# A decoder block on one Trainium2 core: the last quarter of the first MLP product by the seven-product scheme

## The chip, the core and the metric

The kernel runs on one core of a Trainium2 chip. The core has five engines that run their own instruction streams: TensorE (PE in the profile, with its weight loads listed apart as PEld), VectorE (DVE), ScalarE (ACT), GpSimd (POOL) and SyncE (SP). Transfers are issued by SP, ACT and POOL and carried out by 16 DMA engines. The metric is the device time of one launch in microseconds. The time before is 901.49 us, the median of three runs (901.35 to 901.75).

## The reference

One layer of a hybrid decoder, 512 tokens of width 1024, all in float32. Two branches of token mixing (chunked gated linear attention and latent attention) are merged by gates and projected; then follows a squared-ReLU MLP of hidden width 4096:

```
g_gla, g_mla = split(sigmoid(gate_logits + b_gate))       # gate_logits: 2048 columns of h @ w_in
x = layer_norm(alpha * x + (g_gla * y_gla + g_mla * y_mla) @ w_out)
h = layer_norm(...)                                        # the MLP's input, 512 x 1024
x = layer_norm(alpha * h + square(relu(h @ w_ff1)) @ w_ff2)
```

The change touches two products: the last 1024 columns of `gate_logits`, and the last 1024 columns of `h @ w_ff1`.

## The kernel before

**Numbers.** A float32 value is held as two float32r parts, `hi` (a rounded copy, made by ACT) and `lo` (the rest, a subtraction on DVE). A product of two values is three matmuls: hi x hi, hi x lo, lo x hi. A matmul's stationary operand is a 128 x 128 tile; the moving one has up to 512 columns, and the sum goes to a PSUM bank of 128 x 512.

**Weights.** All weight tiles of 512 KB stand in one list, `stream`, in the order of use. `pump(i)`, called where tile i is used, has SP load tiles up to two ahead into a buffer `wraw` (three of them) and splits tiles up to one ahead: ACT copies into `whi` (L185), DVE subtracts into `wlo` (L186), two buffers each. Some tiles of the list come from a tile that is already on the chip (`wq`, loaded earlier, or a sum) instead of from a load.

**Order.** The program is written as generators; `spawn` starts side work, `tick` lets it advance by one step, `finish` runs it to its end. From that program a scheduler fixes the order of the instructions on each engine; an engine then executes its list in order, and waits on semaphores. A tile pool hands out buffers in turn, so an instruction that wants a buffer waits until the last reader of its previous content is done.

**Plain products.** `gemm_fm` (L238 to L240) runs over the 8 tiles of the inner dimension and for each over up to 4 output tiles of 128 columns, three matmuls of 512 tokens each. `gemm_tm` (L271 to L273) is the same with the tokens on the other side.

**Seven-product units.** A product of two matrices can be cut into 2 x 2 quadrants and done by 7 products of quadrants instead of 8, with sums of quadrants on both sides and sums of results. The last 1024 columns of the gate projection are done that way by `gemm_unit("g1")` (L1016 to L1018). Its products come in the order of `FMO`: quadrant 11, quadrant 21, sum t1, quadrant 22, sums t2, t3, t4. Each product of quadrants is 4 inner tiles x 4 output tiles x 3 = 48 matmuls of 256 columns (256 tokens). The sums of weights: t1 and t3 are made by two transfers, a load of one quadrant and, on POOL, a load that adds a second quadrant (L990); t2 and t4 are added by DVE to the tile before, as soon as the tile they add has been split (`u_sum`, L324). A weight quadrant is two tiles of the stream: tile `hf` holds half of its inner tiles, over all 512 columns. Sums of inputs come from `op_sums` (L965 to L972, splits at L111 and L112). Results are combined in `e1`, `e5` and `u2` by a copy on ACT and an addition or subtraction on DVE (L1023 to L1036).

**The MLP.** The hidden width is done in four chunks `ci` of 1024. For chunks 0 to 2 the first product is plain (`gemm_fm`, in blocks of columns), and the second is a seven-product form over 14 steps, `win_f2` (L1268 to L1270). Its weights come through POOL's queue (`win_load`, L1213) one chunk ahead. Its results are copied by ACT into `ev` (L1280) and added to the residual `res` by accumulating transfers on POOL's queue (L1282); `ev` shares a pool of 2 KB buffers with `relu`, `e1`, `e5` and `u2`. ACT's copy into `ev` therefore waits until an earlier transfer out of that buffer has landed. For chunk 3 the first product is two plain blocks of 512 columns; `ev_h` evacuates each output tile: ReLU (ACT, L1296), square into the high part (ACT, L1310), the square again in float32 (POOL, L1311), the difference as the low part (DVE, L1312). Then the last second product, `f2last`, runs as `gemm_tm` with the last layer norm behind it.

Of the kernel before, what the change touches and what calls it, by code (L numbers as in the profile page):

```python
# [19 lines left out]
P = 128  # L20
T = 512
# [31 lines left out]
def tile_hybrid_block(ctx: ExitStack, tc: tile.TileContext, I, out, dbg=None):  # L53
# [108 lines left out]
    def pump(i):  # L162
        while st["dma"] < min(len(stream), i + 1 + DMA_AHEAD):
# [10 lines left out]
            e["raw"] = raw  # L174
        while st["spl"] < min(len(stream), i + 2 + SPLIT_AHEAD):
            e = stream[st["spl"]]
            if st["spl"] > i + e.get("ahead", SPLIT_AHEAD) and not e["res"]:
                break
            nk, n = e["nk"], e["n"]
            hi, lo = [A([P, nk, T * 2 // nk], F32R, w) for w in HOME["a" if e["res"] else e.get("home", "w")]]  # L180
            raw = e["src"]() if "src" in e else e.pop("raw")
            with ExitStack() as gates:
                for g in st["gates"]:
                    gates.enter_context(tc.issue_after(g.ins))
                st["ins"] = act(hi[:, :nk, :n], raw[:, :nk, :n], AF.Copy)  # L185
                vtt(lo[:, :nk, :n], raw[:, :nk, :n], f(hi[:, :nk, :n]), op=ALU.subtract)  # L186
# [121 lines left out]
    UNITS = {"g1": ("w_in", C_G + D)}  # L308

    def plan_src(key, seq, homes):  # L310
        PL[key] = []
# [10 lines left out]
    def u_sum(key, a, to, hf, x):  # L322
        t = WQ[key, (to, hf)] = WQ[key, (a, hf)]
        vtt(t, t, x, op=ALU.add)  # L324


    for key in UNITS:
        PL[key] = []
        for op, _ in FMO:
            for hf in range(2):  # L330
                PL[key].append(len(stream))
                e = {"nk": 2, "n": T, "res": False}
                if op[0] != "t":
                    e["dmas"] = [(slice(0, 2), u_src(key, int(op[0]) - 1, int(op[1]) - 1, hf), None)]
                else:
                    e["src"] = lambda q=(key, (op, hf)): WQ[q]
                if op == "22":
                    e["post"] = lambda raw, q=(key, "t1", "t2", hf): u_sum(*q, raw)
                elif op == "t2":
                    e["post"] = lambda raw, q=(key, "t2", "t4", hf): u_sum(*q, WQ[key, ("21", q[3])])  # L340
                stream.append(e)
    plan_qr(0)
    PL["yg", 0] = plan("w_o_gla", 0, T)

# [22 lines left out]


    FC = 4
    F1 = [((0, 4), (4, 2), (6, 2))] + [tuple((b, 2) for b in range(0, 8, 2))] * 2 + [((0, 4), (4, 4))]  # L370
    WIN = (("11", 0, 0), ("21", 0, 1), ("11", 1, 0), ("21", 1, 1), ("T1", 0, 2), ("T1", 1, 2), ("T2", 0, 3), ("T2", 1, 3),
           ("T4", 0, 4), ("T4", 1, 4), ("22", 0, 5), ("22", 1, 5), ("T3", 0, 6), ("T3", 1, 6))
    fb = 0
    for ci in range(FC):
        nb = 8
        for b, w in F1[ci]:
            PL["f1", ci, b] = plan("w_ff1", (fb + b) * P, w * P, res=(ci == 0 and b == 0), per=8 // w)
        if ci < FC - 1:
            plan_src(("f2", ci), [(op, hf) for op, hf, _ in WIN], HOMES)
        else:  # L380
            plan_zip("f2last", [("w_ff2", 0, fb, True), ("w_ff2", T, fb, True)])
        fb += nb

# [598 lines left out]
            yield  # L982
            ops.append(o)

    def u_load(key, op):
        for hf in range(2):
            t = WQ[key, (op, hf)] = A([P, 2, T], F32, "wq")
            nc.sync.dma_start(t, u_src(key, *{"21": (1, 0)}.get(op, (0, 1)), hf))
            if op != "21":
                nc.gpsimd.dma_start(t, u_src(key, *{"t1": (0, 0), "t3": (1, 1)}[op], hf), accum_op=ALU.add)  # L990

    def gemm_unit(key, ops, evac, after=None):

        bank, e1, e5, u2 = {}, {}, {}, {}
        nk = 2
        for n, (op, ph) in enumerate(FMO):
            items = PL[key][2 * n:2 * n + 2]
            for g in range(2):
                bk = ("a" if ph in (0, 3, 6, 4) else "b", g)
                opens = ph in (0, 2, 1)  # L1000
                if opens:
                    bank[bk] = (PX if ph == 1 else MM)()
                o = bank[bk]
                for hf, it in enumerate(items):
                    pump(it)
                    hi, lo = stream[it]["w"]
                    for pp in range(nk):
                        while len(ops) <= nk * hf + pp:
                            tick(3)
                        xh, xl = ops[nk * hf + pp][ph]  # L1010
                        for a in range(2):
                            c = slice((2 * g + a) * P, (2 * g + a + 1) * P)
                            oa = o[:, a * 256:(a + 1) * 256]
                            first = opens and hf == 0 and pp == 0 and a == 0
                            last = hf == 4 // nk - 1 and pp == nk - 1
                            mm(oa, hi[:, pp, c], xh, start=first, stop=False, skip_group_check=True)  # L1016
                            mm(oa, hi[:, pp, c], xl, start=False, stop=False, skip_group_check=True)  # L1017
                            mm(oa, lo[:, pp, c], xh, start=False, stop=last, skip_group_check=True)  # L1018
                        if pp % 2:
                            tick(3)  # L1020
                if ph == 0:
                    e1[g] = B([P, T], F32, "e1")
                    act(e1[g], o, AF.Copy)  # L1023
                elif ph == 1:
                    vtt(e1[g], o, e1[g], op=ALU.add)
                    evac(0, 0, g, e1[g], None)
                elif ph == 2:
                    e5[g] = B([P, T], F32, "e5")
                    act(e5[g], o, AF.Copy)
                elif ph == 3:  # L1030
                    u2[g] = B([P, T], F32, "u2")
                    act(u2[g], o, AF.Copy)
                    vtt(u2[g], bank["b", g], u2[g], op=ALU.subtract)
                    evac(1, 0, g, u2[g], None)
                elif ph == 6:
                    vtt(e5[g], e5[g], o, op=ALU.subtract)  # L1036
                    evac(1, 1, g, e5[g], None)
                elif ph == 4:
                    evac(0, 1, g, o, None)
            if after:  # L1040
                after(op)


    gt = [None] * NK
# [207 lines left out]
    def win_f2(ci, hid):  # L1252
        bank = {}
        for n, (op, hf, ph) in enumerate(WIN):
# [27 lines left out]
                        nc.gpsimd.dma_start(res[tt + t][:, j * T:(j + 1) * T], e, accum_op=ALU.add)  # L1282
            if n == 9 and ci + 1 < FC - 1:
                win_load(ci + 1)

    WT = {}
    for ci in range(FC):
        nb = 8
        hid = []
# [4 lines left out]
        def ev_h(a, ps):  # L1294
            r = B([P, T], F32, "relu")
            act(r, ps, AF.Relu)  # L1296
            if win:
                if a % 2 == 0:
                    hid.append({"R": A([P, 2, T], F32, "hr")})
                ops = hid[-1]  # L1300
                R = ops["R"]
                act(R[:, a % 2, :], r, AF.Square)
                if a % 2:
                    h1 = A([P, 2, 2, 256], F32R, "h1p")
                    split(R[:, :, :256], h1[:, 0], h1[:, 1])
                    ops[0], ops[1] = [(h1[:, 0, i], h1[:, 1, i]) for i in range(2)]
                    spawn(win_hid(R, ops))
                return
            hh = A([P, 2, T], F32R, "hid0")
            act(hh[:, 0, :], r, AF.Square)  # L1310
            gtt(r, r, r, op=ALU.mult)  # L1311
            vtt(hh[:, 1, :], r, f(hh[:, 0, :]), op=ALU.subtract)  # L1312
            hid.append(hh)
        for b, w in F1[ci]:
            if ci == 0 and b == 0:
                gemm_fm(PL["f1", ci, b], h1T, T, ev_h, toks=slice(256, T), accs=accs)
# [11 lines left out]
            win_f2(ci, hid)  # L1328
        else:
            bg, bb = bcast_row("ln2_g"), bcast_row("ln2_b")  # L1330
            gemm_tm(PL["f2last"], hid, T, ev_res, tts=(0, 1))
            spawn(ln2(0))
            spawn(ln2(1))
# [65 lines left out]
```

## Time and profile before

| what | value |
|---|---|
| median of the runs | 901.49 us (901.35 to 901.75) |
| the profiled execution's own time | 901.97 us |
| its span | 900.2 us |
| instructions | 12161 |
| PE busy | 880.9 us, 98% of the span, 4652 matmuls |
| DVE, ACT, POOL busy | 585.5, 427.3, 178.0 us |

The profile lists each instruction with its start and duration in microseconds of the span, what ended the idle time before it, and what it read and wrote under the program's tile names. Matmuls are pipelined, so that a matmul's listed duration is longer than the distance to the next one's start; distances between starts give the rate. In a row of a group, the number behind x is the count, then follow busy time and mean. `res<-ev` is a transfer from the tile ev to the tile res. "To landing" is the time from a transfer's issue to the end of its last packet. In the list of before, the gate unit runs from 274 to 318 us, the second product of chunk 2 ends at 805 us, the first product of chunk 3 runs from 805 to 848.5 us, and `f2last` begins there.

### The profile page before, as it was taken

The page shows a single profiled execution, that of the slowest core. Times are in us where ns is not written, and L with a number is a line of the kernel's source. Part 1 is how long each engine was busy: PE and PEld are TensorE (multiplying, and loading weights), DVE is VectorE, ACT ScalarE, POOL GpSimd, SP SyncE. Part 2 cuts the span into 40 slices and gives each one's busy share as a digit, 9 for nine tenths or more (in the row PEclk, how much of TensorE's full clock was granted, in tenths as well). Part 3 has the DMA queues.
Part 4 walks back from the last instruction along what each step waited for, and adds up shares of the span by engine and source line. Part 5 has one row for each costly group of instructions (what it writes and reads, how often), then busy time and mean ns, then how long its engine had stood idle before and what let it go on. Part 6 is the DMA issues. An engine that isn't in the chain of part 4 may idle for free.

```text
span 900.2 us, 12161 instructions
## 1 busy us (share of the span) xinstructions
PE 880.9 (98%) x4652; PEld 755.8 (84%) x4652; DVE 585.5 (65%) x953; ACT 427.3 (47%) x729; POOL 178.0 (20%) x196
## 2 busy tenths in 40 slices
PE   5999999999999999999999999999999999999996
PEld 5988888888889988888888888988888888888885
DVE  7835855577876645747756797997557646723565
ACT  5556443443546543445644423466367546733410
POOL 0103442444531010100000002104400520142200
PEclk9999999999999999999999999999999999999999
DMA  7414323216225623121207518005941990594311
GB/s 241 124 47 159 129 65 94 71 47 155 81 71 195 175 88 105 43 60 53 94 24 277 191 49 302 1 1 151 296 115 32 261 243 24 117 209 108 128 68 73
DMA packets 64776, 107.25 MB, mean 119 GB/s; under 512 B 7840, under 2 KB 27680, under 8 KB 64720
## 3 DMA queue, kind: packets, MB, share of 16 engines
q1 hardware_dynamic: 51344, 75.57, 26.3%
q0 software_dynamic: 11456, 27.27, 13.0%
q10 hardware_dynamic: 1920, 3.66, 1.2%
q8 instruction: 36, 0.59, 0.3%
q14 instruction: 20, 0.16, 0.1%
HBM read 89.18 MB, written 4.72 MB: 104 GB/s over the span
## 4 chain that ended last, share of the span: by engine, by line
PE 96%; DVE 2%; DMA 1%; ACT 1%; issue 0%; SPq 0%; DVEq 0%
PE mm L238 14%; PE mm L240 14%; PE mm L239 14%; PE mm L271 7%; PE mm L273 7%; PE mm L272 7%; PE px L1269 2%; PE px L1270 2%; PE px L1268 2%; PE px L723 2%; PE mm L1269 2%; PE mm L1270 2%; PE mm L1268 2%; PE mm L1018 1%; PE mm L1016 1%; PE mm L1017 1%
## 5 line engine op out<-in xcount | busy, mean ns | idle before, releaser
L186 DVE TENSOR_TENSOR wlo<-wraw,whi 128x1024 fp32r<-128x1024 f32 (+1 forms) x102 | 115.3, 1131 | 131.6 <-ACT whi L185 124.0
L185 ACT ACTIVATE whi<-wraw 128x1024 fp32r<-128x1024 f32 (+1 forms) x102 | 98.2, 962 | 109.5 <-PE mm L239 63.3
L238 PE MATMUL mm<-h,whi 128*128 128x512 f32 x352 | 137.6, 392 | 0.0
L239 PE MATMUL mm<-h,whi 128*128 128x512 f32 x352 | 137.3, 390 | 0.0
L240 PE MATMUL mm<-h,wlo 128*128 128x512 f32 x352 | 130.5, 390 | 0.0
L1282 POOL DMA_DIRECT2D res<-ev x48 | 42.1, 1018 | 187.5 <-ACT ev L1280 151.6
L238 PEld LDWEIGHTS mm<-h,whi 128*128 128x128 f32 x352 | 66.0, 188 | 13.5
L240 PEld LDWEIGHTS mm<-h,wlo 128*128 128x128 f32 x352 | 66.0, 188 | 13.5
L239 PEld LDWEIGHTS mm<-h,whi 128*128 128x128 f32 x352 | 66.1, 188 | 13.3
L272 PE MATMUL mm<-wlo,h 128*128 128x512 f32 x128 | 50.3, 393 | 0.0
L273 PE MATMUL mm<-whi,h 128*128 128x512 f32 x128 | 50.1, 392 | 0.0
L271 PE MATMUL mm<-whi,h 128*128 128x512 f32 x128 | 49.7, 403 | 0.0
L185 ACT ACTIVATE xh<-wraw 128x1024 fp32r<-128x1024 f32 (+1 forms) x28 | 27.1, 985 | 36.8 <-PE mm L273 16.5
L662 POOL TENSOR_TENSOR rp<-rp 128x256 f32<-128x256 f32 x32 | 31.6, 987 | 61.2 <-ACT E L667 44.8
L1296 ACT ACTIVATE relu<-mm 128x512 f32<-128x512 f32 x32 | 18.8, 595 | 49.3 <-PE mm L240 49.2
L186 DVE TENSOR_TENSOR wlo<-wq,whi 128x1024 fp32r<-128x1024 f32 x20 | 24.5, 1225 | 24.2 <-ACT whi L185 24.2
L391 POOL TENSOR_TENSOR mv<-mv,mhalf 128x1 f32<-128x1 f32 x4 | 4.6, 1154 | 172.4 <-DVE mv L390 172.4
L186 DVE TENSOR_TENSOR xl<-wraw,xh 128x1024 fp32r<-128x1024 f32 (+1 forms) x28 | 31.2, 1128 | 8.9 <-ACT xh L185 8.7
L669 DVE TENSOR_TENSOR M<-E,qk 128x512 f32<-128x512 f32 x32 | 27.8, 868 | 14.1 <-ACT E L667 14.1
L667 ACT ACTIVATE E<-rp 128x512 f32<-128x512 f32 x32 | 20.4, 638 | 24.9 <-POOL rp L663 24.9
L663 POOL TENSOR_TENSOR rp<-rp 128x256 f32<-128x256 f32 x32 | 28.2, 883 | 8.9 <-ACT q L692 6.7
L273 PEld LDWEIGHTS mm<-whi,h 128*128 128x128 f32 x128 | 24.0, 188 | 5.0
(405 smaller groups left out, 2415.3 us busy)
## 6 DMA issues: line engine op xcount, KB each, us to landing
wraw<-in_w_ff_dram SPq DMA_DIRECT2D x40, 512.0 KB, 4.5
wraw<-in_w_in_dram SPq DMA_DIRECT2D x38, 512.0 KB, 3.5
wq<-in_w_ff_dram POOLq DMA_DIRECT2D x24, 512.0 KB, 9.4
res<-ev POOLq DMA_DIRECT2D x48, 256.0 KB, 6.6
wraw<-in_w_o_gla_dram SPq DMA_DIRECT2D x8, 512.0 KB, 3.8
wraw<-in_w_o_mla_dram SPq DMA_DIRECT2D x8, 512.0 KB, 3.5
wraw<-in_w_out_dram SPq DMA_DIRECT2D x8, 512.0 KB, 3.9
wq<-in_w_in_dram SPq DMA_DIRECT2D x6, 512.0 KB, 5.5
```

Of the source, the lines that this page charges most:

```text
L185: st["ins"] = act(hi[:, :nk, :n], raw[:, :nk, :n], AF.Copy)
L186: vtt(lo[:, :nk, :n], raw[:, :nk, :n], f(hi[:, :nk, :n]), op=ALU.subtract)
L238: mm(o, hi[:, c], xh, start=first, stop=False)
L239: mm(o, hi[:, c], xl, start=False, stop=False)
L240: mm(o, lo[:, c], xh, start=False, stop=last)
L271: mm(o, xh, hi[:, :n], start=opens, stop=False, skip_group_check=share)
L272: mm(o, xh, lo[:, :n], start=False, stop=False, skip_group_check=share)
L273: mm(o, xl, hi[:, :n], start=False, stop=last, skip_group_check=share)
L1268: mm(o, xh[:, c], hi[:, pp], start=opens, stop=False, skip_group_check=True)
L1269: mm(o, xh[:, c], lo[:, pp], start=False, stop=False, skip_group_check=True)
L1270: mm(o, xl[:, c], hi[:, pp], start=False, stop=hf == 1 and pp == 1, skip_group_check=True)
L1282: nc.gpsimd.dma_start(res[tt + t][:, j * T:(j + 1) * T], e, accum_op=ALU.add)
```

## The change

Three things change.

1. In a seven-product unit a weight quadrant's two tiles are now its two column halves (`g`), each with all four inner tiles, loaded in rows of 1 KB instead of 2 KB. A tile then serves 24 matmuls into one output bank, and the next tile the other bank. The sums of weights on DVE are put behind the last low-half subtraction queued before them (`issue_after(st["lo"].ins)`).
2. The last chunk's first product is done by a unit "f1" of the same form: 336 matmuls of 256 columns in the place of 192 of 512. Its input sums are made by `op_sums` on `h1T`, spawned in step 10 of the third `win_f2`. In the same `win_f2` POOL issues the two transfers for t1 in step 8, SP is told to fetch up to quadrant 22 in step 9, and POOL loads quadrant 21 in step 11. That quadrant is kept, and DVE adds it to t2 for t4 instead of loading it again. The transfers for t3 are issued on POOL after product 21.
3. The evacuation of that chunk, `ev_u`, does its float32 square on DVE instead of POOL, in generators that step beside the products; `Halves` lets `f2last` wait for each quarter of the hidden tile.

```diff
-    def u_src(key, i, j, hf):
-        return src[:, 4 * hf + i:4 * hf + i + 3:2, c0 + j * T:c0 + (j + 1) * T]
+    def u_src(key, i, j, g):
+        c0 += j * T + g * 256
+        return src[:, i:8:2, c0:c0 + 256]
...
+        with tc.issue_after(st["lo"].ins):
+            vtt(t, t, x, op=ALU.add)
...
-    F1 = [((0, 4), (4, 2), (6, 2))] + [tuple((b, 2) for b in range(0, 8, 2))] * 2 + [((0, 4), (4, 4))]
+    F1 = [((0, 4), (4, 2), (6, 2))] + [tuple((b, 2) for b in range(0, 8, 2))] * 2 + [()]
...
+            plan_unit("f1")
...
+            for g in range(2):
+                bk = ("a" if ph in (0, 3, 6, 4) else "b", g)
+                o, it = bank[bk], PL[key, op, g]
+                pump(it)
+                hi, lo = stream[it]["w"]
+                for k in range(4):
+                    xh, xl = ops[k][ph]
+                    for a in range(2):
+                        c = slice(a * P, (a + 1) * P)
+                        oa = o[:, a * 256:(a + 1) * 256]
+                        mm(oa, hi[:, k, c], xh, start=opens and k == 0 and a == 0, stop=False, skip_group_check=True)
+                        mm(oa, hi[:, k, c], xl, start=False, stop=False, skip_group_check=True)
+                        mm(oa, lo[:, k, c], xh, start=False, stop=k == 3, skip_group_check=True)
...
+            if ci == FC - 2 and n == U0:
+                t_h1.append(spawn(h1_sums()))
+            if ci == FC - 2 and n == U2:
+                fetch(PL["f1", "22", 0] + 1)
+            if ci == FC - 2 and n == U1:
+                u_load("f1", "t1", nc.gpsimd.dma_start)
+            if ci == FC - 2 and n == U3:
+                u_load("f1", "21", nc.gpsimd.dma_start)
...
+    U0, U1, U2, U3 = 10, 8, 9, 11
...
-            hh = A([P, 2, T], F32R, "hid0")
-            act(hh[:, 0, :], r, AF.Square)
-            gtt(r, r, r, op=ALU.mult)
-            vtt(hh[:, 1, :], r, f(hh[:, 0, :]), op=ALU.subtract)
...
+            def ev_u(j, i, g, ps, sb):
+                def later():
+                    for _ in range(1 + 4 * i):
+                        yield
+                    r = ps if sb else B([P, T], F32, "relu")
+                    act(r, ps, AF.Relu)
+                    hh = A([P, 2, 2, 256], F32R, "hid0")
+                    act(hh[:, 0], r.rearrange("p (a c) -> p a c", a=2), AF.Square)
+                    yield
+                    vtt(r, r, r, op=ALU.mult)
+                    vtt(hh[:, 1], r.rearrange("p (a c) -> p a c", a=2), f(hh[:, 0]), op=ALU.subtract)
+                    hts[j, i, g] = hh
+                spawn(later())
+            def after1(op):
+                if op == "21":
+                    u_load("f1", "t3", nc.gpsimd.dma_start)
+            gemm_unit("f1", hops, ev_u, after1)
```

More of the change, by code (lines that the diff above doesn't have):

```diff
@@ L1001, in gemm_unit @@
                 if opens:
[L1002 to L1020, printed above, removed]
+                    bank[bk] = (PX if ph == 1 else (pb or MM) if ph == 2 else MM)()
@@ L1296, in ev_h @@
             act(r, ps, AF.Relu)
[L1297 to L1308, printed above, removed]
-            hh = A([P, 2, T], F32R, "hid0")
[L1310 to L1313, printed above, removed]
+            if a % 2 == 0:
+                hid.append({"R": A([P, 2, T], F32, "hr")})
+            ops = hid[-1]
+            R = ops["R"]
+            act(R[:, a % 2, :], r, AF.Square)
+            if a % 2:
+                h1 = A([P, 2, 2, 256], F32R, "h1p")
+                split(R[:, :, :256], h1[:, 0], h1[:, 1])
+                ops[0], ops[1] = [(h1[:, 0, i], h1[:, 1, i]) for i in range(2)]
+                spawn(win_hid(R, ops))
         for b, w in F1[ci]:
```

90 lines of the change are left out of this document (58 added, 32 removed).

## The prediction

> **What bounds the kernel.** I read the page's busy shares and slices first, then the chain that ended last, then windows around the two places that the change touches.
>
> ```profile
> PE 880.9 (98%) x4652; PEld 755.8 (84%) x4652; DVE 585.5 (65%) x953; ACT 427.3 (47%) x729; POOL 178.0 (20%) x196
> ...
> PE   5999999999999999999999999999999999999996
> ...
> PEclk9999999999999999999999999999999999999999
> ...
> PE 96%; DVE 2%; DMA 1%; ACT 1%; issue 0%; SPq 0%; DVEq 0%
> ```
>
> PE is busy 98% of the span, in every slice but the first and last, at full clock, and 96% of the chain is PE. So the time follows the PE time of the work, plus any gap that another engine forces into it. The profiled execution took 901.97 us for a span of 900.2 us (1.8 us lie around it), 0.48 us above the median of 901.49 us. I work out a difference in the span and take it from the median.
>
> ```profile
> 775.00:805.00 30.00, 30.00 (x134) 24.85 (x133) 15.72 (x14) 16.05 (x22) 10.37 (x12) 1.00 0.92 202
> 805.00:849.00 44.00, 44.00 (x196) 36.42 (x194) 14.64 (x12) 15.46 (x23) 9.04 (x9) 1.00 0.48 132
> 849.00:893.00 44.00, 43.53 (x215) 36.87 (x213) 30.81 (x46) 8.06 (x10) 7.73 (x7) 1.00 0.20 72
> ```
>
> The columns are the length, then the busy time of PE, PEld, DVE, ACT and POOL, the clock, the DMA share and GB/s. The tail of the third second-MLP product (775 to 805), the first product's last 1024 columns (805 to 849) and the start of the last product have no idle PE. A shorter first product is thus gained in full if its operands come in time. DVE, ACT and POOL have about half their time or more free until 849, but the DMA engines are 92% busy before 805.
>
> **1. Fewer, narrower matmuls.** PE rows of both shapes, start and duration, and the weight loads of the narrow ones:
>
> ```profile
> 805.02 0.39 PE L238 MATMUL mm<-h,whi 128*128 128x512 f32 x1
> ...
> 806.38 0.39 PE L238 MATMUL mm<-h,whi 128*128 128x512 f32 x1
> ...
> 285.86 0.28 PE L1016 MATMUL px<-h,whi 128*128 128x256 f32 x1
> ...
> 287.06 0.28 PE L1016 MATMUL px<-h,whi 128*128 128x256 f32 x1
> ...
> L1018 PEld LDWEIGHTS mm<-h,wlo x32: 186/192/192, 274.4 to 317.7; 128*128 128x128 f32 x32
> ```
>
> Durations overlap, so starts are what counts. Six starts of 512 columns lie in 805.02 to 806.38: 0.2267 us each. Ten of 256 columns lie in 285.86 to 287.06: 0.120 us each. The old form is 2 blocks x 4 row tiles x 8 input tiles x 3 = 192 matmuls: 43.5 us, as the window shows. The new one is 7 products x 48 = 336 matmuls: 40.3 us. **Term: -3.2 us.** Seven eighths of the arithmetic would be -5.4 us; the narrow form gives back 2.2 us of it (0.120 against 0.113).
>
> The Trainium skill (TensorE: Matmul & The Clock Gate, section Back-to-back issue gap) gives sustained spacings of about 81 ns at 128 columns and 131 ns at 512 for streams with a weight load per matmul. Interpolated, 256 columns would take some 98 ns, an estimate from that page, and this term would turn to 336 x 0.098 - 192 x 0.131 = +7.8 us. The rows above differ on both widths, and they decide.
>
> **2. The gate unit's split by columns.** PE and DVE around the unit's only real gap:
>
> ```profile
> 311.53 0.28 PE L1017 MATMUL mm<-h,whi 128*128 128x256 f32 x1
> 312.29 0.38 PE L1018 MATMUL mm<-h,wlo 128*128 128x256 f32 x1 [0.48 <-DVE wlo L186]
> ...
> 310.41 0.69 DVE L1036 TENSOR_TENSOR e<-e,mm 128x512 f32<-128x512 f32 x1 [1.87 <-PE mm L1018]
> 311.01 1.22 DVE L186 TENSOR_TENSOR wlo<-wq,whi 128x1024 fp32r<-128x1024 f32 x1
> ```
>
> The matmul that should start 0.12 us after 311.53 starts at 312.29, 0.64 us late, and the next one 0.10 us later than the pace: 0.74 us. It waited for the low half of the next weight tile (wlo, 311.01 + 1.22). DVE runs in order, and that subtract stood behind e (L1036), which waited 1.87 us for the whole product to end. Split by rows, a product's two outputs end together. Split by columns, the first ends after 24 matmuls, 2.88 us earlier than the second; e (0.69) and the subtract (1.22) then fit before the next tile is needed. **Term: -0.7 us**, between -0.74 and 0. The weight sums stand behind the last subtract instead of ahead of it, so they delay nothing. Loads now have 1 KB rows instead of 2 KB; the accumulating ones are costed below. Nothing else in the unit moves.
>
> **3. More work on ACT and DVE.**
>
> ```profile
> L186 DVE TENSOR_TENSOR wlo<-wraw,whi 128x1024 fp32r<-128x1024 f32 x82 | 103.1, 1258 | 111.5 <-ACT whi L185 103.9 <-PE px L817 3.6 <-PE px L880 3.4
> L185 ACT ACTIVATE whi<-wraw 128x1024 fp32r<-128x1024 f32 x82 | 86.8, 1059 | 82.7 <-PE mm L239 43.1 <-PE mm L273 14.1 <-DMA wraw<-in_w_ff_dram 6.8
> ...
> L1221 DVE TENSOR_TENSOR T<-wq,wq 128x1024 f32<-128x1024 f32 x12 | 14.5, 1220 | 0.9 <-DMA wq<-in_w_ff_dram 0.9
> ...
> L965 DVE TENSOR_TENSOR hraw<-h 128x512 f32<-128x512 f32 x8 | 6.2, 803 | 0.0
> ...
> L112 DVE TENSOR_TENSOR sh<-hx,sh 128x512 fp32r<-128x512 f32 x8 | 5.7, 740 | 3.1 <-ACT sh L111 3.1
> ...
> L1311 POOL TENSOR_TENSOR relu<-relu 128x512 f32<-128x512 f32 x8 | 10.3, 1301 | 35.4 <-ACT hid L1310 35.4
> L1312 DVE TENSOR_TENSOR hid<-relu,hid 128x512 fp32r<-128x512 f32 x8 | 10.3, 1312 | 11.8 <-POOL relu L1311 11.8
> ...
> L1296 ACT ACTIVATE relu<-mm 128x512 f32<-128x512 f32 x8 | 4.8, 595 | 8.6 <-PE mm L240 8.4
> ...
> L1036 DVE TENSOR_TENSOR e<-e,mm 128x512 f32<-128x512 f32 x2 | 1.4, 686 | 1.9 <-PE mm L1018 1.9
> ```
>
> Columns are count, then busy us, mean ns, idle before. The new unit splits 14 weight tiles where 8 were split: 6 more at 1.26 on DVE and 1.06 on ACT. DVE adds four weight sums (the shape of L1221, 1.22 each), eight sums of inputs (L965, 0.80), sixteen half-width ones (about half that, 0.4), eight low halves (0.74), six combinations like L1036 (0.69) and eight squares taken over from POOL, where L1311 took 1.30; on DVE a tensor operation of that shape takes 0.69. The subtract L1312 stays; its 1.31 was taken beside POOL's multiply, so it may shrink toward 0.69. In sum 7.6 + 4.9 + 6.4 + 6.4 + 5.9 + 4.1 + 5.5 = 41 us more DVE work, beside 15.7 + 14.6 = 30.3 us busy in the 74 us from 775 to 849. That is 96%, though a part of the evacuation falls behind 845. ACT gains 6.4 (splits) + 4.8 (input sums) + 3.6 (copies of banks) = 15 us on 31.5 and stays far from full. A tile is used for 24 x 0.120 = 2.88 us, and its successor needs ACT 1.06 and DVE 1.26 in turn, 0.56 us less. The gate unit kept this pace with the same kinds of work, and its one gap is that of step 2. I take **0**; the high end is 0.5 us for four of the products, +2 us.
>
> **4. The POOL queue: the unknown.** The new loads go through POOL's queue, among the accumulating copies of ev into res (L1282). Its order after the change, from 785 on: the base of t1, both halves; two copies; then POOL waits for the first base to land and issues its accumulate, quadrant "21" in two halves, a copy, the other accumulate, a copy (the pair that began at 791.15 before), eight more issues of copies, and last the base and the accumulates of t3. No form with both was run. Rows: copies when the queue is light; 512 KB loads and copies when it is full; accumulating loads.
>
> ```profile
> 784.90 0.86 POOL L1282 DMA_DIRECT2D res<-ev  x1 [1.71 <-ACT ev L1280]
> ...
> 791.15 0.86 POOL L1282 DMA_DIRECT2D res<-ev  x1 [0.85 <-ACT ev L1280]
> ...
> DMA to landing us min/median/max: 3.3/5.0/7.5
> ...
> DMA to landing us min/median/max: 7.1/10.5/13.2
> ...
> 644.13 0.60 ACT L1280 ACTIVATE ev<-mm 128x512 f32<-128x512 f32 x1 [1.19 <-DMA res<-ev]
> 645.91 0.60 ACT L1280 ACTIVATE ev<-px 128x512 f32<-128x512 f32 x1 [1.18 <-DMA res<-ev]
> 647.69 0.60 ACT L1280 ACTIVATE ev<-px 128x512 f32<-128x512 f32 x1 [1.19 <-DMA res<-ev]
> ...
> 287.62 2.54 POOL L990 DMA_DIRECT2D wq<-in_w_in_dram  x2 [8.45 <-PE px L1018]
> ...
> DMA to landing us min/median/max: 8.5/9.3/10.1
> ```
>
> The full queue (622 to 652) lands things in issue order. Eight loads issued 622.7 to 630.3 land 7.1 to 13.2 us after issue, and copies land so that ev, which waits for the buffer of an earlier one, runs at 644.13, 645.91, 647.69: 1.78 us for each piece. Two accumulates issued together at 287.62, 1.27 us apart, took 8.5 and 10.1 us: the second landed about 2.9 us behind the first. Here the last earlier copy (issued 784.90) lands some 3.5 us later, at 788.4, near the light queue's 3.3. Ten pieces then follow, up to the second copy of that pair: 8 x 1.75 + 2 x 2.9 = 19.8, so it lands at 808.2.
>
> Its buffer is what the last ev of this second product waits for, whose matmuls end at 805.02. ACT is in order: behind this ev (0.60) stand half of an input's split (0.6) and the high half of "21", first column half (1.06). So ACT finishes at 810.5 and DVE's low half at about 811.8. PE reaches "21" after 48 x 0.120 us, at 810.8, and its third matmul, the first with the low half, at 811.0. **Term: +1.2 us** (0.8 by this sum, and 0.4 for four steps from engine to engine), between 0 (1.4 us per piece: landing at 803.8) and +3.0 (3.5 us per accumulate and POOL held until a base lands late: 810.4).
>
> The second deadline is t3. Its base is issued when the copies before it have their buffers, about 812, lands by 824, and the accumulates land about 830 and 833. ACT wants the halves by 833.8 - 2.3 = 831.5 and 834.4, later by any earlier stall. That is a cover of 1 us: cost 0, and 1 to 2 us if the queue is slower by a tenth.
>
> SP's own loads are not moved past anything, but they share the engines. Of the first row below (the whole run) and the other two (630 to 652), the last column is the median time to landing:
>
> ```profile
> wraw<-in_w_ff_dram SPq DMA_DIRECT2D x40, 512.0 KB, 4.5
> ...
> res<-ev POOLq DMA_DIRECT2D x11, 256.0 KB, 10.2
> wraw<-in_w_ff_dram SPq DMA_DIRECT2D x3, 512.0 KB, 11.2
> ```
>
> SP's 512 KB loads took 11.2 us there instead of 4.5. The Trainium skill (Trainium Kernel Development and Optimization, Key Constraints) says that all queues use the same 16 DMA engines and interleave; this row agrees. Loads of "11" are issued by about 786 and wanted near 797 and 802, those of "22" by 801 for 819, so 11 us is still hidden. Those of the last product are issued as each split tile frees its buffer, about one product (5.76 us) ahead: with 4.5 us the cover is about 1 us, and a late one would cost what it is late. One load of "21" instead of two saves transfers, not time.
>
> **5. The rest.** f2last reads the new halves as they are made; evacuation of the last output (ACT 0.6 + 0.6, DVE 0.69 + 0.69) ends about 848, and f2last uses it last, so 0. LN2 and the output transfers follow PE unchanged.
>
> **Sum:** -3.2 - 0.7 + 0 + 1.2 = -2.7 us: 899.3 for an execution like the profiled one, **898.8 us** against the median.
>
> **Rivals.**
> - Full gain: the queue is quick enough and ACT never waits. -3.2 - 0.7: 897.6 us. For it: in the light queue copies land 3.3 to 7.5 us after issue. Against it: six 512 KB loads come on top.
> - Pace: the split chain loses 0.3 to 0.6 us in most products, or the gate unit gains nothing. For it: DVE at 96%, cover of 0.56 us. Against it: the gate unit's single gap. -3.2 + 1.2 + 2 to 3: 900 to 902.5 us, no change.
> - Slower, the queue's backlog. If a piece takes 2.2 us and an accumulate 3 or more, that copy lands at 812 to 815; "21" stalls 4.5 to 7.5 us, and t3, behind ten more pieces, costs 2 to 4 us more. -3.9 + 6.5 to 11.5: 904 to 909 us. It decides from a landing past 809.5 on. For it: DMA already at 92%. Against it: 1.78 in the fullest stretch of this run.
> - Weight loads set the pace of narrow matmuls: LDWEIGHTS takes 0.192 us, more than the 0.120. 336 x 0.19 = 64 us, +20 us: 922 us. Against it: the 0.120 us starts with those very loads.
>
> **How the numbers follow.** Forecast with a stall of 0.3 to 2.1 us (897.9 to 899.7): 0.44. Full gain: 0.13. Pace: 0.2. Backlog: 0.21. Weight loads: 0.02. What a measurement can tell from no change is about 0.2%, 1.8 us: faster 0.57 (the first two), same 0.2, slower 0.23. The range runs from 897.2 (full gain, less the 0.4 us between the lowest and the highest of the runs shown) to 904, where the backlog begins; 0.2 is left out above it. The forecast's own range is 897.6 to 899.9.
>
> **What would show it.** Step 1: starts 0.120 us apart over 40.3 us, no 512-column matmul from 805 to 845. Step 2: no PE gap near 311, e runs before wlo. Step 3: no PE gap put down to DVE wlo within the unit, DVE above 80% there. Step 4: the first matmuls of "21" near 811 wait about 1 us for wlo or whi, whose ACT stood behind ev waiting for DMA res<-ev; t3's high half waits for no DMA. The prediction is wrong if that copy lands past 810, if t3's accumulates land past 834, or if PE shows gaps at every second tile.

## The result, and the profile after

The changed kernel takes 906.35 us, the median of 6 runs (905.37 to 909.06); the kernel before, on the same chip, 901.42 us (6 runs, 900.98 to 901.75). The ratio is 1.0060, with an interval of 1.0045 to 1.0076: slower by 4.9 us, where 2.7 us faster was forecast. The profiled execution took 905.63 us for a span of 903.5 us, 3.3 us more span than before. What follows explains that one execution; it lies 0.7 us below the median.

The page of the changed kernel, its busy shares, clock and chain:

```profile
PE 879.5 (97%) x4796; PEld 761.3 (84%) x4796; DVE 617.3 (68%) x1009; ACT 440.2 (49%) x749; POOL 178.1 (20%) x198
...
PE   6999999999999999999999999999999999988996
...
PEclk9999999999999999999999999999999999998999
...
PE 92%; DMA 4%; DVE 2%; issue 1%; ACT 1%; POOL 0%; SPq 0%; DVEq 0%; POOLq 0%; ACTq 0%
```

PE has less work and is no longer busy throughout: two more slices of 22.6 us show a digit below 9, one of them at a lower clock. On the chain, DMA has gone from 1% to 4%. The same place in windows (columns as before: length, busy time of PE, PEld, DVE, ACT, POOL, clock, DMA share, GB/s):

```profile
775.00:805.00 30.00, 30.00 (x140) 25.09 (x139) 26.61 (x41) 16.86 (x25) 14.13 (x16) 1.00 0.93 217
805.00:809.30 4.30, 4.30 (x38) 4.24 (x36) 1.85 (x3) 0.60 (x1) 0.85 (x1) 1.00 1.17 231
809.30:815.20 5.90, 0.14 (x2) 0.00 (x0) 0.69 (x1) 2.04 (x4) 0.85 (x1) 0.76 1.12 251
815.20:819.20 4.00, 3.46 (x14) 3.17 (x15) 3.06 (x3) 2.46 (x5) 3.51 (x6) 0.50 1.09 194
819.20:852.00 32.80, 32.80 (x266) 32.34 (x265) 27.91 (x31) 21.82 (x29) 4.15 (x4) 1.00 0.61 136
```

Nearly all of the loss lies in 10 us. PE stands still from 809.3 to 815.2, between quadrant 11 and quadrant 21, and then works for 4 us at a granted clock of 0.50. The matmuls there, and ACT's row of instructions that PE waited for:

```profile
809.16 0.28 PE L1023 MATMUL mm<-h,wlo 128*128 128x256 f32 x1
815.27 0.58 PE L1021 MATMUL px<-h,whi 128*128 128x256 f32 x1 [5.83 <-ACT whi L188]
815.66 0.41 PE L1022 MATMUL px<-h,whi 128*128 128x256 f32 x1
816.53 0.58 PE L1023 MATMUL px<-h,wlo 128*128 128x256 f32 x1 [0.46 <-DVE wlo L189]
...
817.56 0.41 PE L1021 MATMUL px<-h,whi 128*128 128x256 f32 x1
817.77 0.41 PE L1022 MATMUL px<-h,whi 128*128 128x256 f32 x1
...
819.23 0.28 PE L1023 MATMUL px<-h,wlo 128*128 128x256 f32 x1
```

```profile
806.62 0.60 ACT L1291 ACTIVATE ev<-px 128x512 f32<-128x512 f32 x1 [3.07 <-PE mm L1023]
813.16 0.60 ACT L1291 ACTIVATE ev<-px 128x512 f32<-128x512 f32 x1 [5.94 <-DMA res<-ev]
813.66 0.62 ACT L111 ACTIVATE sh<-hx 128x512 fp32r<-128x512 f32 x1
814.18 1.05 ACT L188 ACTIVATE whi<-wq 128x1024 fp32r<-128x1024 f32 x1
```

The copy that the last `ev` waited for:

```profile
L1293 POOL DMA_DIRECT2D res<-ev x1: 2144/2144/2144, 798.4 to 798.4; - x1
...
DMA to landing us min/median/max: 14.6/14.6/14.6
```

It is the place that step 4 named. The last `ev` of the second product waits 5.94 us for a buffer, that is, for an earlier copy into `res` to land: it was issued at 798.45 and landed at 813.08, 0.08 us before this `ev` starts. The `ev` before it, at 806.62, also starts 0.08 us after such a landing (806.54), so its 3.07 us were most likely the same wait, though the profile names PE. Half of an input's split and the high half of "21" stand behind it on ACT, and PE stands behind those. Quadrant "21" itself had been on the chip since 805.3 us by the trace.

The account of the span: the gate unit starts at 273.60 instead of 274.32, so 0.7 us are won in the part ahead that the change does not touch (in the profile of experiment 7's control, which does not have the change, it starts at 273.80, so most of it is a difference between executions). The gate unit itself is 0.8 us shorter (42.81 against 43.58 from its first matmul to the next stage), and the first product's matmuls 3.2 us. Against that, the gaps beyond the pace between 760 and 903 add up to 8.3 us: 6.0 of standstill, 0.75 for the low half at 816.53, 1.3 for starts 0.21 us apart instead of 0.120 until 819.23, and 0.3 between the first two matmuls after the standstill. Another -0.3 is what the other terms leave over: -0.7 - 0.8 - 3.2 + 8.3 - 0.3 = +3.3 us.

### The profile page after: what moved, and what is told of

It is laid out like the page before. It is cut to its first block, busy times and chain, and to the rows that moved or that the text cites. A ratio compares the mean times of both kernels' runs of the same rounds, so it can differ in the third digit from the quotient of the medians.

```text
span 903.5 us, 12536 instructions
## 1 busy us (share of the span) xinstructions
PE 879.5 (97%) x4796; PEld 761.3 (84%) x4796; DVE 617.3 (68%) x1009; ACT 440.2 (49%) x749; POOL 178.1 (20%) x198
## 4 chain that ended last, share of the span: by engine, by line
PE 92%; DMA 4%; DVE 2%; issue 1%; ACT 1%; POOL 0%; SPq 0%; DVEq 0%; POOLq 0%; ACTq 0%
PE mm L241 12%; PE mm L243 12%; PE mm L242 12%; PE mm L274 7%; PE mm L275 7%; PE mm L276 7%; DMA res<-ev 2%; PE mm L1022 2%; PE mm L1023 2%; PE mm L1021 2%; PE px L1280 2%; PE px L1279 2%; PE px L1281 2%; PE px L731 2%; PE mm L1280 1%; PE mm L1279 1%
## 5 line engine op out<-in xcount | busy, mean ns | idle before, releaser
L189 DVE TENSOR_TENSOR wlo<-wraw,whi 128x1024 fp32r<-128x1024 f32 (+1 forms) x98 | 110.4, 1127 | 108.6 <-ACT whi L188 101.0
L241 PE MATMUL mm<-h,whi 128*128 128x512 f32 x288 | 112.7, 392 | 0.0
L242 PE MATMUL mm<-h,whi 128*128 128x512 f32 x288 | 112.4, 390 | 0.0
L243 PE MATMUL mm<-h,wlo 128*128 128x512 f32 x288 | 107.1, 390 | 0.0
L243 PEld LDWEIGHTS mm<-h,wlo 128*128 128x128 f32 x288 | 53.9, 188 | 11.1
L241 PEld LDWEIGHTS mm<-h,whi 128*128 128x128 f32 x288 | 54.0, 188 | 11.0
L242 PEld LDWEIGHTS mm<-h,whi 128*128 128x128 f32 x288 | 54.1, 188 | 10.8
L189 DVE TENSOR_TENSOR wlo<-wq,whi 128x1024 fp32r<-128x1024 f32 x30 | 36.7, 1224 | 19.9 <-ACT whi L188 19.8
L670 POOL TENSOR_TENSOR rp<-rp 128x256 f32<-128x256 f32 x32 | 31.7, 990 | 61.1 <-ACT E L675 44.8
L188 ACT ACTIVATE whi<-wq 128x1024 fp32r<-128x1024 f32 x30 | 31.7, 1057 | 19.6 <-PE mm L1022 10.8
L1021 PE MATMUL mm<-sh,whi 128*128 128x256 f32 x128 | 36.2, 283 | 0.0
L1022 PE MATMUL mm<-sh,whi 128*128 128x256 f32 x128 | 36.2, 283 | 0.0
L1023 PE MATMUL mm<-sh,wlo 128*128 128x256 f32 x128 | 36.2, 283 | 0.0
```

Source lines behind the costliest of these rows:

```text
L189: st["lo"] = vtt(lo[:, :nk, :n], raw[:, :nk, :n], f(hi[:, :nk, :n]), op=ALU.subtract)
L241: mm(o, hi[:, c], xh, start=first, stop=False)
L242: mm(o, hi[:, c], xl, start=False, stop=False)
L243: mm(o, lo[:, c], xh, start=False, stop=last)
L1021: mm(oa, hi[:, k, c], xh, start=opens and k == 0 and a == 0, stop=False, skip_group_check=True)
L1022: mm(oa, hi[:, k, c], xl, start=False, stop=False, skip_group_check=True)
```

## The experiments

The theory after the result was: the copies of the third second product land late in a queue that now carries six more loads, and ACT waits for their buffers. The rivals: the accumulating loads are what is slow; the order on POOL's queue is; or DVE's load would hold the pace below the forecast even without this stall.

**1. The gate unit alone.** The last 1024 columns of the first MLP product stay plain; only the split by columns and the place of the sums are kept. The old evacuation, with the square on POOL, is back too.

```diff
-    F1 = [((0, 4), (4, 2), (6, 2))] + [...] * 2 + [()]
+    F1 = [((0, 4), (4, 2), (6, 2))] + [...] * 2 + [((0, 4), (4, 4))]
...
-            plan_unit("f1")
...
```

> The gate unit split by columns, the last chunk's first product plain as before. Theory (the loss is all in the new unit, from the POOL queue): the gap of 0.74 us near 311 is gone and nothing else moves, so 901.4 - 0.7 = 900.7 us. Rival (the 1 KB rows or the moved weight sums cost something in the gate unit): 901.4 or more.

Measured: 901.07 us (11 runs, 900.46 to 901.68) against 901.72, ratio 0.9993 (0.9985 to 1.0002); span 899.2. The -0.65 us is the size of step 2, but its interval holds 1: the time alone does not show it. The trace of the changed kernel does. Its matmuls at the place of the old gap run at the pace:

```profile
311.37 0.28 PE L1021 MATMUL mm<-h,whi 128*128 128x256 f32 x1
...
311.97 0.28 PE L1023 MATMUL mm<-h,wlo 128*128 128x256 f32 x1
```

Five steps in 0.60 us, with no wait. The loss thus belongs to the unit "f1", with its loads and its evacuation.

**2. The loads on SP's queue.** The bases of t1 and t3 and quadrant "21" go through SP's queue; the accumulating loads have to stay on POOL's.

```diff
-                u_load("f1", "t1", nc.gpsimd.dma_start)
+                u_load("f1", "t1")
...
-                u_load("f1", "21", nc.gpsimd.dma_start)
+                u_load("f1", "21")
...
-                    u_load("f1", "t3", nc.gpsimd.dma_start)
+                    u_load("f1", "t3")
```

> As changed, but the plain loads of the new unit (bases of t1 and t3, quadrant 21) are issued on SP's queue; only the accumulating loads stay on POOL's. Theory (it is the order of POOL's queue that makes the copy before the last ev land late, 813 us): four loads fewer stand ahead of that copy, about 4 x 1.75 = 7 us, it lands near 806, the stall at quadrant 21 falls from 7 us to under 2, and the time is 898 to 901 us. Rival (the 16 DMA engines are full in that stretch, whatever the queue): the copy still lands past 811 and the time stays at 904 to 907 us.

**3. The same, without the accumulating loads.** The sums t1 and t3 then hold one quadrant only.

```diff
-            if op != "21":
+            if op != "21" and key != "f1":
                 nc.gpsimd...
```

> As the run before with the loads on SP, and without the new unit's four accumulating loads, so t1 and t3 hold one quadrant each and the output is not the reference's. POOL's queue carries only the copies, as before the change. Theory (queue): no stall is left, 901.4 - 0.7 - 3.2 = 897.5 us. Rival (DVE at 96% or the split chain cannot keep 2.88 us per tile): gaps at wlo remain, and the time is 899 us or more.

Measured: 903.28 us (10 runs, 900.44 to 905.03; ratio 1.0016, 1.0005 to 1.0027) and 903.33 us (10 runs, 900.68 to 905.15; 1.0014, 1.0005 to 1.0023). Both win 3 us on the changed kernel, and the second wins nothing on the first: with the other loads on SP's queue, the accumulating loads cost nothing that the time shows. Experiment 2 was expected at 898 to 901 us and experiment 3 at 897.5; both came out slower. In experiment 2 the copy that had landed at 813.1 landed at 807.1, as its theory of the queue's order has it (near 806), and the stall at "21" fell to 1.0 us. But PE stood still at another place, 798 to 800.4, in both. PE and ACT in experiment 3, which has neither accumulating loads nor new loads on POOL's queue:

```profile
798.00 0.39 PE L1279 MATMUL px<-whi,xh 128*128 128x512 f32 x1
800.43 0.50 PE L1280 MATMUL px<-wlo,xh 128*128 128x512 f32 x1 [2.05 <-DVE wlo L189]
800.77 0.40 PE L1281 MATMUL px<-whi,xl 128*128 128x512 f32 x1
801.01 0.48 PE L1279 MATMUL px<-whi,xh 128*128 128x512 f32 x1
801.29 0.63 PE L1280 MATMUL px<-wlo,xh 128*128 128x512 f32 x1
801.72 0.63 PE L1281 MATMUL px<-whi,xl 128*128 128x512 f32 x1
```

```profile
783.54 0.60 ACT L1291 ACTIVATE ev<-px 128x512 f32<-128x512 f32 x1 [3.23 <-DMA res<-ev]
784.03 1.05 ACT L188 ACTIVATE xh<-T 128x1024 fp32r<-128x1024 f32 x1
...
792.45 0.60 ACT L1291 ACTIVATE ev<-mm 128x512 f32<-128x512 f32 x1 [3.20 <-DMA res<-ev]
792.94 1.05 ACT L188 ACTIVATE xh<-wq 128x1024 fp32r<-128x1024 f32 x1
```

`ev` waits for copies here too, three times around 3 us from 783 on (3.23, 2.61 and 3.20), and each time a split `xh` stands behind it. DVE idles for `xh` as long (2.93 us before its row at 789.27, 3.52 before 794.02); the input sums for "f1" then come late in DVE's order, and the low half that PE wants at 798.2 is begun only at 799.16. The three copies issued from 780.6 to 788.6 land 7.0 to 7.9 us after issue; the three from 782.3 to 787.3 in the kernel before took 3.5 to 6.2 us. New in this stretch are the 512 KB loads on SP's queue, so these delay POOL's copies too. Changing the queue moved the place of the stall and cut the loss against the kernel before from 4.9 to 1.6 us. The rival of experiment 3, that DVE cannot hold the pace, named the place where PE waits (`wlo`) and the time (899 us or more), but not the reason: DVE had idled for ACT.

**4. The copies replaced by additions on POOL.** The 16 results of that second product are added into `res` by POOL as a tensor operation.

```diff
-                        nc.gpsimd.dma_start(res[...], e, accum_op=ALU.add)
+                        if ci == FC - 2:
+                            gtt(rr, rr, e, op=ALU.add)
+                        else:
+                            nc.gpsimd.dma_start(rr, e, accum_op=ALU.add)
```

> As changed, all loads on POOL's queue, but the third second product's copies into the residual are additions by POOL (16 of 128x512, about 1.3 us each by POOL's multiply) instead of accumulating transfers. Theory (ACT waits for a copy's landing, not the weights for theirs): ev is free 1.3 us after it is written, quadrant 21 is on the chip near 800, no stall at 811, 897.5 to 899 us. Rival 1 (the weights themselves are late): the stall stays above 4 us. Rival 2 (POOL's additions slow DVE, which is nearly full): gaps at wlo of 0.5 us per product, 900 to 903 us.

Measured: 915.17 us (4 runs, 912.66 to 915.56), ratio 1.0142 (1.0128 to 1.0156). No `ev` waits for a transfer any more, but DVE became slow. Groups of POOL and DVE from 775 to 812 in this run, and then those of DVE in the changed kernel:

```profile
L1295 POOL TENSOR_TENSOR res<-res,ev 128x512 f32<-128x512 f32 x12 | 21.9, 1840 | 51.7 <-ACT ev L1291 51.7
...
L189 DVE TENSOR_TENSOR xl<-wq,xh 128x1024 fp32r<-128x1024 f32 x2 | 5.3, 2702 | 0.0
L112 DVE TENSOR_TENSOR sh<-hx,sh 128x512 fp32r<-128x512 f32 x4 | 4.9, 1226 | 0.0
...
L980 DVE TENSOR_TENSOR hx<-hraw 128x256 f32<-128x256 f32 x3 | 3.8, 1251 | 0.0
```

```profile
L112 DVE TENSOR_TENSOR sh<-hx,sh 128x512 fp32r<-128x512 f32 x6 | 3.9, 686 | 0.3 <-ACT sh L111 0.2
...
L189 DVE TENSOR_TENSOR xl<-wq,xh 128x1024 fp32r<-128x1024 f32 x2 | 2.4, 1222 | 0.0
...
L980 DVE TENSOR_TENSOR hx<-hraw 128x256 f32<-128x256 f32 x4 | 1.7, 419 | 0.0
```

These operations take 2.70 us in the mean instead of 1.22, 1.23 instead of 0.69, 1.25 instead of 0.42; some other groups of the window did not grow (the sums of L973 take 0.68 in both). PE then waited for ACT and DVE at six places, 10.7 us together. The time lies above everything expected: the second rival had the mechanism, at 900 to 903 us. This run says nothing on the copies, but on where such an addition must not be done. The Trainium skill (SBUF — State Buffer, section SBUF: two separate sides) says that DVE with two SBUF inputs and a GpSimd operation share a pair of ports as a lock held for the whole instruction; rows that grow, by less than the 1.84 us that one addition of POOL's takes, agree with that.

**5. No copies at all.** The copies of that second product are left out (its results are missing in the output); every load stays as it is in the changed kernel.

```diff
-                        nc.gpsimd.dma_start(res[...], e, accum_op=ALU.add)
+                        if ci < FC - 2: nc.gpsimd.dma_start(res[...], e, accum_op=ALU.add)
```

> As changed, with the third second product's 16 copies into the residual left out (ev is still written, nothing reads it, and the output lacks that product). All loads of the new unit stay on POOL's queue. Theory (the copies fill queue and engines, and through ev's buffers hold ACT and then DVE): no gap near 800 or 811, and 901.4 - 0.7 - 3.2 = 897.5 us. Rival (DVE's input sums, or the loads by themselves, are late): a gap of 2 us or more at wlo or whi remains, 900 us or more.

Measured: 897.35 us (4 runs, 897.23 to 897.55) against 901.5, ratio 0.9954 (0.9939 to 0.9968). The window over what was the stall (columns as above):

```profile
803.50:847.00 43.50, 43.50 (x352) 42.92 (x351) 36.48 (x43) 28.54 (x39) 2.59 (x2) 1.00 0.43 109
```

PE has no gap, at full clock, with DVE at 84%. This is the price of the rival "full gain" (-3.2 - 0.7: 897.6) to 0.3 us. The copies of the third second product, or the wait for them, are the cause, and steps 1 to 3 hold with the pace as forecast. Whether it is their volume on the DMA engines or the wait of `ev` for their landing, this run cannot tell; experiments 6 and 9 can.

**6. Three pairs of results added by DVE.** Where step 5, 7 or 9 of the 14 ends (the results T1, T2 and T4), DVE adds the PSUM bank into `res`; `ev` and the copies of these six results go, the other ten remain.

```diff
+                    if ci == FC - 2 and n in (5, 7, 9):
+                        for tt, j in (...)[ph]:
+                            rr = res[tt + t][:, j * T:(j + 1) * T]
+                            vtt(rr, rr, o, op=ALU.subtract if ph == 4 else ALU.add)
+                        continue
                     e = B([P, T], F32, "ev")
```

> As changed, but in the third second product the results T1, T2 and T4 are added to the residual by DVE straight from the PSUM bank (6 x 0.69 us), so that ACT writes 6 ev fewer and POOL's queue has 6 copies fewer; the four of the first two products, quadrant 22's two and T3's four stay transfers. Theory: ev's buffers are free when wanted, quadrant 21's copy-bound stall goes, the time is 897.5 to 899 us. Rival (DVE, nearly full, is the bound as soon as ACT is not): gaps at wlo near 800 of 1 us or more and 900 to 902 us.

**7. The same additions in the kernel before**, as a control for what they are worth by themselves (its diff is that of experiment 6).

> Control: the kernel before, with the six additions on DVE of the runs above and nothing of the change. PE has no gap in that stretch before, so if the additions only take away the wait that the change brought, this is 901.5 us, the same as before. Rival (the additions gain by themselves, and the change is still a loss under them): 898 to 900 us.

Measured: experiment 6 takes 898.17 us (4 runs, 897.44 to 899.02), ratio 0.9963 (0.9948 to 0.9978): faster than both kernels. The control takes 901.15 us (10 runs, 900.54 to 901.50), 0.9992 (0.9982 to 1.0001): nothing that can be measured. So the change is worth about 3.0 us (901.15 - 898.17; 2.9 when each is first compared with the kernel before as measured beside it) when the wait for the copies is out of the way. Experiment 6's waits of PE from 775 to 850, and the landing of six of its ten copies (the code stands five lines lower here):

```profile
PE px L1023 <- DVE wlo L189: 0.6, 1, 0.6
```

```profile
L1298 POOL DMA_DIRECT2D res<-ev x6: 847/1144/1865, 798.3 to 805.3; - x6
...
DMA to landing us min/median/max: 11.3/12.9/14.1
```

These copies land as late as those of the changed kernel (12.8 us after issue in the median, of six issued 797.1 to 813.6), and the only gap is 0.6 us for a low half. The queue is as slow; there is just no `ev` near "21" that needs its buffer back. This speaks against the mere volume on the DMA engines as the cause.

**8. Variants of experiment 6.** With the new loads on SP's queue as in experiment 2; with the layer-norm parameters' loads held back to about 798; with a fourth pair added by DVE:

```diff
-                u_load("f1", "t1", nc.gpsimd.dma_start)
+                u_load("f1", "t1")
...
```

```diff
-            bg, bb = bcast_row("ln2_g"), bcast_row("ln2_b")
+            with tc.issue_after(st["ins"].ins):
+                bg, bb = bcast_row("ln2_g"), bcast_row("ln2_b")
```

```diff
-                    if ci == FC - 2 and n in (5, 7, 9):
+                    if ci == FC - 2 and n in (5, 7, 9, 11):
```

> The run before with the plain loads of the new unit on SP's queue too. If POOL's queue still matters with 6 copies fewer, this is faster than the run before by up to 2 us; if only the volume on the engines and ev's buffers matter, the two agree within 0.1%.

> The DVE additions, and the two 512 KB loads of the last norm's parameters (issued at 772 and 776 us, the second landing at 783) held back until some 798 us. Theory of engine volume: 1 MB less ahead of the copies of 776 to 786, ACT's evs there run up to 2 us sooner, 0 to 1 us gained over the DVE additions alone. Rival: those loads had landed before the stretch that matters, no difference.

> The additions on DVE for quadrant 22's result as well (8 of 0.69 us; only the first two products' and T3's results are copied). Two copies fewer in the queue and two evs fewer on ACT: the 0.7 us gap left at quadrant 21 goes, 897.3 us. Rival: DVE's extra 1.4 us near 800 delays the low half there, 898 us or more.

Measured: 897.62 us (7 runs; ratio 0.9965, 0.9953 to 0.9976), 897.88 us (6 runs; 0.9968, 0.9953 to 0.9983) and 899.01 us (6 runs; 0.9969, 0.9957 to 0.9980). Their intervals cover each other and that of experiment 6. The queue of the loads no longer matters, nor do the parameters' loads. The fourth pair adds nothing: 897.3 was expected, and the time fell where its rival had it (898 or more), with one wait of PE left, 0.8 us for the high half of "21".

**9. More buffers, all transfers kept.** The pool that `ev` shares gets 24 buffers instead of 22, and another pool gives up one of 24.

```diff
-... name="pb", bufs=22
+... name="pb", bufs=24
...
-... else ("A", 24)
+... else ("A", 23)
```

> As changed, every transfer kept; the pool of ev gets two buffers more (24 for 22), paid for by one 4 KB buffer less in the large pool (23 for 24). Theory (what counts is ev's buffer, not the volume): the last ev then waits for the copy two places earlier, which landed at 806.5 instead of 813.1, so the stall at quadrant 21 falls from 7 us to about 1 and the time to 898 to 900 us, with copies landing as late as before. Rival (volume on the engines): 904 us or more. The smaller large pool may hold up loads, which would show as a gap of its own.

Measured: 905.59 us (4 runs, 904.14 to 907.71), ratio 1.0044 (1.0030 to 1.0058): no better than the changed kernel's 1.0060 within the intervals. It was expected at 898 to 900 us; the time fell where the rival had it (904 or more). The profiled execution is the slowest of these, 907.71 us, span 905.8. Its waits from 800 to 850:

```profile
ACT whi L188 <- DMA wq<-in_w_ff_dram: 12.3, 4, 7.5
POOL res L1293 <- DMA res<-ev: 12.0, 3, 9.3
...
PE mm L1021 <- ACT u L1037: 4.3, 1, 4.3
...
PE px L1023 <- DVE wlo L189: 0.8, 1, 0.8
...
PE px L1021 <- ACT whi L188: 0.4, 1, 0.4
ACT ev L1291 <- DMA res<-ev: 0.4, 1, 0.4
```

The mechanism of the buffers holds, though not its time: `ev` waits for 0.4 us instead of 5.9, and the stall at "21" falls to 0.4 + 0.8 us. What is left there waits for "21" itself, whose first half landed only at 809.9. But a new stall of 4.3 us comes with t3, and the lowered clock behind it costs another 3.1 us. POOL's own issue of a copy waits up to 9.3 us for earlier copies into `res`, t3's loads stand behind it, and ACT waits up to 7.5 us for t3's weights. The copy of a bank, `u`, which PE needs, stands behind that split:

```profile
835.16 0.28 PE L1023 MATMUL mm<-sh,wlo 128*128 128x256 f32 x1
839.78 0.58 PE L1021 MATMUL mm<-sh,whi 128*128 128x256 f32 x1 [4.34 <-ACT u L1037]
840.16 0.41 PE L1022 MATMUL mm<-sh,whi 128*128 128x256 f32 x1
...
818.24 3.51 POOL L1293 DMA_DIRECT2D res<-ev  x4 [9.31 <-DMA res<-ev]
```

So two waits hang on the one slow queue, and taking away the first only uncovers the second. In the changed kernel t3's second half landed at 839.5, and its split began at 840.7; that it was in time only because of the 8 us lost before is worked out from these times, and experiment 9 bears it out. What POOL waits for is the earlier copy into the same part of `res`: its issues at 806.39, 808.07 and 818.24 each follow the landing of that copy (805.83, 807.54 and 817.71) by 0.5 us. No run tried it without that order. The run changes two pools at once; no load waits for a buffer in the listing, so the smaller pool does not show.

## Why the prediction was wrong

- **Step 1 (-3.2 us) was right.** The 0.120 us pace stands in every undisturbed stretch, and experiment 5 gives the full gain's time to 0.3 us. The rival of the weight loads (922 us) is out.
- **Step 2 (-0.7 us) was right** as the trace shows it (-0.8, the gap is gone); experiment 1's time agrees, within noise.
- **Step 3 (0) was right, too pessimistic in its load.** From 775 to 849 DVE was 87% busy in experiment 5 (64.4 of 74 us) and not 96%: over the whole run it got 31.8 us more work (617.3 against 585.5), not 41. The only wait of PE for a low half from 770 to 850 in the changed kernel is the one at the stall, and in experiment 5 there is none. The rival "pace" is out.
- **Step 4 (+1.2 us) is the step that failed**: it measured 6.7 us (6.0 of standstill, 0.75 for the low half), and 8.1 us with the lowered clock behind it. Its chain was right: the copy's landing, then `ev`, half of a split, the high half, PE; from `ev`'s start to PE's it took 2.1 us. The landing was wrong, 813.1 instead of 808.2, above the high end of 810.4. And PE reached "21" at 809.3, not 810.8, because of the 0.7 and 0.8 us won ahead, while the landing did not move with it. By the trace's landing times its 4.9 us are these. The queue's last earlier copy landed 790.9, not 788.4 (+2.5): I took the light queue's 3.5 us, but this copy was in flight with 512 KB loads of both queues and took 6.7. The first new load landed 3.4 us behind it, not 1.75 (+1.6). The two accumulating loads took 3.3 and 4.3 us in their turn, not 2.9 each (+1.8). The seven other pieces took 11.2 us instead of 12.3 (-1.0). So not one price but four assumptions of the landing were off, three of them on the same side, which a range of +0 to +3.0 did not hold. This account is read from one trace; experiment 2 tested only a part of it, the loads in front.
- **The second deadline** (t3, "a cover of 1 us") was real. Its accumulates landed at 833.6 and 839.5, not at 830 and 833, past the 834 that the prediction had set as a sign; the stall at "21" hid it. Experiment 9 shows it: where that stall goes, t3 stalls 4.3 us.
- **Left out: the lowered clock after the standstill**, 1.3 us.
- **The rivals.** "Backlog" is what happened: the result lies in its 904 to 909, past its deciding landing of 809.5, though with the stall at one place instead of two. At 0.21 it had too small a chance. What spoke against it, 1.78 us per piece, held for the plain pieces (1.6 in the mean, at a DMA share of 1.08 from 791 to 813, as in 630 to 652 before). Its price for a piece (2.2 us) was too high, its price for an accumulate (3 or more) right; the rest of the delay came from the first two assumptions, which it did not name.

## What to carry to other kernels

When loads are moved into a stretch, price first who waits there for buffers that transfers give back: the new loads were in time, and what they delayed was an old copy whose buffer ACT needed. A landing time holds only for what was in flight beside it (here 3.5 us for a copy without new loads, 6.7 with them); each piece of a queue's forecast needs a row with the same company, and the errors add up. And if one wait is removed, the next deadline on the same queue has to be worked out as well (experiment 9), while taking transfers out of it (experiments 5 and 6) met both deadlines here.

## What the runs showed of the hardware

**The clock falls after a standstill.** After 5.8 us of idle PE the granted clock was 0.50 from 815.2 to 819.2 us, and starts lay 0.21 us apart; after the 4.3 us of experiment 9 it was 0.51 for 6.5 us. Experiment 3's 2.05 us of idle time was enough, though with a delay: its first starts lie 0.24 to 0.34 us apart (the pace is 0.23), then 0.43. The window row of experiment 9, and then those of experiment 3 (columns as above):

```profile
839.70:846.20 6.50, 6.42 (x28) 6.14 (x29) 3.77 (x5) 3.47 (x6) 0.00 (x0) 0.51 0.02 4
...
797.90:800.40 2.50, 0.48 (x3) 0.06 (x1) 2.50 (x5) 2.50 (x5) 0.86 (x2) 1.00 0.71 125
800.40:804.40 4.00, 3.97 (x11) 3.10 (x12) 3.97 (x9) 2.06 (x5) 0.88 (x1) 0.60 0.77 131
804.40:813.00 8.60, 8.60 (x60) 7.96 (x59) 8.46 (x16) 5.18 (x9) 5.06 (x6) 0.99 0.86 150
```

A gap of 0.6 us (experiment 6) left the clock alone. The Trainium skill (TensorE: Matmul & The Clock Gate, section What's actually happening) gives half the clock after an idle window of about 3.4 us, until about 3.4 us of work have passed. The 4 us at 0.50 roughly agree with it; the 6.5 us of experiment 9 are nearly twice as long, and the 2.05 us of idle time that sufficed are shorter than such a window.

**POOL's additions slow DVE.** The means of the DVE groups shown for experiment 4 grew by 0.5 to 1.5 us beside POOL's tensor additions of 1.84 us, while DVE's own additions from PSUM into SBUF in experiment 6 took 0.68 us and cost nothing that the time shows.
